# Two k stacks copied from ScalarE's queue, and x's first tile issued ahead of the parameter rows, in a two-layer encoder

## The chip, the cores and the metric

The kernel runs on one core of one Trainium2 chip. The metric is the device time of one execution in microseconds (us). Before the change it is 2428.93 us, the median of three runs (2426.2, 2428.93 and 2428.98).

## The reference, cut to what matters

`h` is 1024 positions by 1024 channels, all float32. Two layers each project `h` to q, k, v (8 heads, two components of 32 channels for q and k, 64 for v) and to u of a Fourier group, attend, mix and normalise, and then run a SwiGLU feed-forward.

```python
h = layer_norm(x, ln_in_g, ln_in_b)
for l in range(DEPTH):                      # DEPTH = 2
    proj = jnp.einsum('bsd,de->bse', h, w_in[l])        # q | k | v | u, 512 columns each
    a = diff_attention(q, k, v, lam, lam_init, subln_g[l])
    f = fourier_mix(u, w_f[l], b_f[l])
    mix = jnp.einsum('bse,ed->bsd', jnp.concatenate([a, f], axis=-1), w_o[l])
    h = layer_norm(ALPHA * h + mix, ln1_g[l], ln1_b[l])
    h = layer_norm(ALPHA * h + swiglu(h, w_gu[l], w_down[l]), ln2_g[l], ln2_b[l])

# diff_attention, for each head: two softmaxes over the same v
s = einsum('bqhcd,bkhcd->bhcqk', q, k) * scale - slope * |qpos - kpos|
p = softmax(s);  a = p[:, :, 0] - lam * p[:, :, 1];  o = a @ v;  o = rms_norm(o) * subln_g * (1 - lam_init)
```

## The kernel before, in words

Every matmul that must keep float32 accuracy is made of three: an operand is split into a high part (`hi`, rounded) and a low part (`lo`, the rest), and `mm3` (L137 to L139) multiplies hi by hi, hi by lo and lo by hi. ScalarE makes `hi`, VectorE or GpSimd makes `lo` by a subtraction (`split`, L127). `hTh` and `hTl` hold the transposed activations.

**The start.** SyncE's queue loads five small parameter rows (`load_rows`, gain and shift of the first norm, b_f, subln_g), then x's first tile in two halves, then four weight tiles of v, then x's other tiles. `spread_ln` (L199) transposes the parameter rows (PE, L201), ScalarE and GpSimd widen two of them (L209, L211), and 16 transposes (L213) spread gain and shift over all partitions in two PSUM tiles. `enter_norm` normalises a tile: statistics on VectorE (L229 to L233), one power on GpSimd (L234), a multiplication by the spread gain out of PSUM on VectorE (L236), a scaling on ScalarE (L238), and the addition of the shift (L240 for tile 0). Each normalised tile is stored to `h_dram` and transposed.

**The first pair of heads in a layer.** `proj_qk` (L293) projects q and k of two heads: PE makes a 128x512 half in a bank `mm`, ScalarE evicts `hi` (tile `st`) and VectorE `lo` (tile `su`). Then it builds stacks: for each of four components `c`, a tile `stk` (q: hi, hi, lo, lo of 32 channels, on 4 x 32 partitions) and a tile `stq` (k: hi, lo, hi, lo), so that one 128-row matmul gives all product terms of a score. (The pool names are crossed: `stk` holds q, `stq` holds k.) Each stack takes four copies of 32 x 1024 float32 (128 KB) from SBUF to SBUF, all issued through `load` (L101, L102), that is by SyncE's queue. In the first pair of layer 0 the stacks of c = 0 and 1 are `stk_708`/`stq_713` and `stk_718`/`stq_723`; in layer 1 they are `stk_11741`/`stq_11746` and `stk_11751`/`stq_11756`.

After k's last half, `proj_v` (L266) makes the last three tiles of v in layer 0 and in layer 1 (24 matmuls of 256 columns each, into a bank `mm`; tiles `mm_748`, `mm_776`, `mm_804` in layer 0, the last one is `mm_11837` in layer 1). There are two `mm` banks, so `mm_804` can begin when `mm_748` has been evicted: ScalarE's cast (L129) and then VectorE's subtraction (L132) for `v_773`.

**Attention.** For each block of 128 queries and each component, `scores` (L387, matmul L392) makes a 128x1024 tile `S` with two 512-column matmuls, `bias_min` adds the ALiBi distance and takes the row's minimum on VectorE (L400), and `expo` takes the exponential on ScalarE (L410). PE fills the time between scores with projections of later pairs (`mm_852` is the first), each step held behind the scores by `tc.issue_after`. Two `S` tiles exist.

**What sets the order.** Each engine runs its instructions in a fixed order, which the build works out from a simulated timeline of all the engines; a queue's DMAs are issued in that order too. The build also hands eight completion counters round to all DMAs of all queues in the scheduled order (`DMAHW0` to `DMAHW7` in the rows of the order below), and a DMA waits until the last one on its counter has landed.

Of the kernel before, what the change touches and what calls it, by code (L numbers as in the profile page):

```python
# [27 lines left out]
HD = 32  # L28
# [31 lines left out]
def f32(t):  # L60
    return t.bitcast(F32)
# [3 lines left out]
def encoder(ctx: ExitStack, tc: tile.TileContext, x, ln_in_g, ln_in_b, w_in, lam_params, subln_g,  # L65
            w_f, b_f, w_o, ln1_g, ln1_b, w_gu, w_down, ln2_g, ln2_b, dist_c, dft_c, grp_c, qsc_c, out):
    nc = tc.nc
# [7 lines left out]
    def nm(s):  # L75
        cnt[0] += 1
        return f"{s}_{cnt[0]}"
# [3 lines left out]
    def blk(tag, shape=(P, 1024), dt=F32):  # L81
        if tag == "s":
            swap[0] ^= 1
            tag = ("su", "st")[swap[0]]
        return sb.tile(list(shape), dt, tag=tag, name=nm(tag), bufs=BUFS[tag])
# [6 lines left out]
    def bank(tag=None):  # L92
        if tag is None:
            alt[0] ^= 1
            tag = ("mm", "tr")[alt[0]]
        return ps.tile([P, 512], F32, tag=tag, name=nm(tag), bufs=2)

    def dbank():
        return ps.tile([P, 1024], F32, tag="S", name=nm("S"), bufs=2)

    def load(o, i):  # L101
        nc.sync.dma_start(out=o, in_=i)  # L102
# [24 lines left out]
    def split(hi, lo, src, hi_eng, lo_eng, note=None):  # L127
        if hi_eng is nc.scalar:
            a = nc.scalar.copy(hi, src)  # L129
        else:  # L130
            a = hi_eng.tensor_copy(out=hi, in_=src)
        b = lo_eng.tensor_tensor(out=lo, in0=src, in1=f32(hi), op=ALU.subtract)  # L132
        if note is not None:
            note[1:] = a, b
# [55 lines left out]
    def load_rows():  # L190
        t = blk("on", (P, P))
        for j, v in enumerate((ln_in_g, ln_in_b)):
            load(t[j * ND:j * ND + ND, :], v.rearrange("(j p) -> j p", p=P))
        load(t[2 * ND:3 * ND, :], b_f.rearrange("l (g p) -> (l g) p", p=P))
        for half in range(2):
            load(t[3 * ND:NR, half * VD:(half + 1) * VD], subln_g)
        return t

    def spread_ln(t):  # L199
        pt = bank("tr")  # L200
        nc.tensor.transpose(pt[:, 0:NR], t[0:NR, :], ident[0:NR, 0:NR])  # L201
        cols = blk("on", (P, NR))
        nc.scalar.copy(cols, pt[:, 0:NR])
        ob, og = dbank(), dbank()
        for k, o in ((0, og), (1, ob)):
            w = blk("stq", (P, ND, P))
            col = cols[:, k * ND:k * ND + ND].unsqueeze(2).broadcast_to([P, ND, P])
            if k:
                nc.gpsimd.tensor_copy(out=w, in_=col)  # L209
            else:  # L210
                nc.scalar.copy(w, col)  # L211
            for j in range(ND):
                nc.tensor.transpose(o[:, j * P:(j + 1) * P], w[:, j, :], ident)  # L213
        b = blk("E")
        nc.scalar.copy(b, ob)
        nc.gpsimd.tensor_copy(out=bfT.rearrange("p l g -> p (l g)"), in_=cols[:, 2 * ND:3 * ND])
        for l in range(DEPTH):
            nc.gpsimd.tensor_scalar(out=subg[:, l:l + 1], in0=cols[:, 3 * ND + l:3 * ND + l + 1],
                                    scalar1=math.sqrt(VD) * (1.0 - LAM_INIT[l]), scalar2=1.0, op0=ALU.mult,
                                    op1=ALU.mult)  # L220
        return og, b, ob
# [34 lines left out]
    def load_v(l):  # L256
        ts = []
        for k in range(4):
            t = blk("E", (P, 2, 2, VH), F32R)
            raw = blk("raw", (P, 2, VH))  # L260
            load(raw, w_in[l, k * 256:(k + 1) * 256, 2 * ATT:2 * ATT + VH].rearrange("(a p) c -> p a c", p=P))
            split(t[:, 0], t[:, 1], raw, nc.scalar, nc.vector if k % 2 and l == 0 else nc.gpsimd)
            ts.append(t)
        return ts
# [12 lines left out]
    def load_w128(l, c0, tag="w"):  # L277
        wh = blk(tag, (P, ND, P), F32R)
        wl = blk(tag, (P, ND, P), F32R)
        for part in range(2):  # L280
            raw = blk("raw", (P, 4, P))
            load(raw, w_in[l, part * 512:part * 512 + 512, c0:c0 + P].rearrange("(a p) c -> p a c", p=P))
            split(wh[:, part * 4:part * 4 + 4, :], wl[:, part * 4:part * 4 + 4, :], raw, nc.scalar, nc.gpsimd)
        return wh, wl

    def proj_t(wh, wl, half, o):
        sl = slice(half * 512, half * 512 + 512)
        for dt in range(ND):
            anchor[1] = mm3(o, wh[:, dt, :], wl[:, dt, :], hTh[:, dt, sl], hTl[:, dt, sl], dt == 0, dt == ND - 1)
            if dt < ND - 1:  # L290
                yield

    def proj_qk(l, pair, stacks):  # L293
        srcs = []
        parts = [(qk, half) for qk in range(2) for half in range(2)]
        if pair == 0:
            parts = [(qk, half) for half in ((1, 0) if l else (0, 1)) for qk in range(2)]
        ready = {}
        for n, (qk, half) in enumerate(parts):
            if qk not in ready:  # L300
                wh, wl = load_w128(l, qk * ATT + pair * P, "aT" if pair == 0 and qk else "w")
                ready[qk] = wh, wl, blk("s", (P, S), F32R), blk("s", (P, S), F32R)
            wh, wl, hi, lo = ready[qk]
            o = bank("mm")
            sl = slice(half * 512, half * 512 + 512)
            yield from proj_t(wh, wl, half, o)
            if qk == 0:
                sc = qsc[:, pair:pair + 1]
                nc.scalar.activation(hi[:, sl], o, AF.Copy, scale=sc)
                nc.vector.scalar_tensor_tensor(out=lo[:, sl], in0=o, scalar=sc, in1=f32(hi[:, sl]),  # L310
                                               op0=ALU.mult, op1=ALU.subtract)
            else:
                split(hi[:, sl], lo[:, sl], o, nc.scalar, nc.vector)
            if n < 3:
                yield "part"
        for qk in range(2):
            wh, wl, hi, lo = ready[qk]
            srcs.append((hi, hi, lo, lo) if qk == 0 else (hi, lo, hi, lo))
        for c in range(4):
            for qk in range(2):  # L320
                t = blk(("stk", "stq")[qk], (P, S), F32R)
                for j in range(4):
                    load(f32(t[j * HD:(j + 1) * HD, :]), f32(srcs[qk][j][c * HD:(c + 1) * HD, :]))
                stacks[qk].append(t)
        yield

# [193 lines left out]
    def attention(l, vs, dist, first):  # L520
# [6 lines left out]
        for h in range(NH):  # L527
            for qt in range(NT):
                if qt % QW == 0:
# [3 lines left out]
                               "z": []})  # L533
                n += 1
        plan = [[proj_qk(l, 1, stacks[1]), proj_vt(l, 2, vs), proj_u(l, 0)],
                [proj_qk(l, 2, stacks[2]), proj_vt(l, 3, vs), proj_u(l, 1)],
                [proj_qk(l, 3, stacks[3]), proj_u(l, 2)],
                [fourier(l)]]
        hs = []
# [556 lines left out]
    rs = [blk("v") for _ in range(NT)]  # L1096
    for i in range(NT):
        if i == 0:
            rows_ = load_rows()
            for c in (slice(0, D // 2), slice(D // 2, D)):  # L1100
                load(rs[i][:, c], x[i * P:(i + 1) * P, c])
            gb = spread_ln(rows_)
            wv = load_v(0)
        else:
            load(rs[i], x[i * P:(i + 1) * P, :])
# [94 lines left out]
```

## Time and profile before

| | |
|---|---|
| median of three runs | 2428.93 us (2426.2 to 2428.98) |
| the profiled execution | 2429.76 us |
| its span, first to last instruction | 2427.5 us |
| mean granted TensorE clock | 0.988 |
| PE busy | 2339.9 us, 96% of the span |
| VectorE, GpSimd, ScalarE busy | 1850.9, 1809.8, 1212.5 us |
| DMA moved | 187.60 MB, mean 77 GB/s |

PE, PEld, DVE, ACT, POOL and SP are TensorE's matmuls, its weight loads, VectorE, ScalarE, GpSimd and SyncE. A time in a row is counted from the first instruction of the span. An L and a number is the line of the kernel. In a timeline, the bracket at the end is the idle time of that engine ahead of the instruction, and what ended it. The granted clock is 1.00 at 2.4 GHz and 0.50 at 1.2 GHz.

### The profile page before, as it was taken

How to read it: one execution, taken by the hardware profiler on the slowest of the kernel's cores; microseconds unless marked ns; L12 is line 12 of the kernel's file. 1: busy time of each engine (PE TensorE's matmuls, PEld its weight loads, DVE VectorE, ACT ScalarE, POOL GpSimd, SP SyncE). 2: the span in 40 equal slices, each digit the busy share in tenths (PEclk: the TensorE clock that was granted, in tenths of full speed). 3: DMA queues.
4: the chain of work that ended last, by engine and by line, in shares of the span. 5: the costliest groups of instructions: out<-in, count | busy, mean ns of one | idle time of the engine just before them, and what ended most of it. 6: DMA issues, size and time to landing. Idle time of an engine off the chain costs nothing.

```text
span 2427.5 us, 33266 instructions
## 1 busy us (share of the span) xinstructions
PE 2339.9 (96%) x11649; PEld 1947.2 (80%) x11649; DVE 1850.9 (76%) x2930; ACT 1212.5 (50%) x2203; POOL 1809.8 (75%) x1378
## 2 busy tenths in 40 slices
PE   7999998999999999999999999989999999999997
PEld 6888876777888888888788888777878888888886
DVE  6587888556688888888768788884566888888878
ACT  4577777524343343434437777774243343434442
POOL 4476778656798888888535777784678888888873
PEclk9999999999999999999999999999999999999999
DMA  6542242421121111121324233325011211111112
GB/s 236 144 102 65 75 105 101 115 81 48 44 61 53 57 53 57 53 61 53 102 87 102 74 77 94 113 66 174 14 53 47 62 58 57 53 57 53 53 35 100
DMA packets 187919, 187.60 MB, mean 77 GB/s; under 512 B 24912, under 2 KB 148200, under 8 KB 187752
## 3 DMA queue, kind: packets, MB, share of 16 engines
q1 hardware_dynamic: 187752, 185.47, 26.2%
q8 instruction: 93, 1.52, 0.3%
q14 instruction: 74, 0.61, 0.1%
HBM read 128.01 MB, written 23.86 MB: 63 GB/s over the span
## 4 chain that ended last, share of the span: by engine, by line
PE 81%; DVE 8%; issue 3%; POOL 3%; ACT 2%; DMA 2%; SPq 1%; DVEq 0%; POOLq 0%; ACTq 0%
PE mm L137 10%; PE mm L139 10%; PE mm L138 10%; PE S L137 7%; PE S L138 7%; PE S L139 7%; PE tr L137 6%; PE tr L139 6%; PE tr L138 6%; PE mm L450 4%; PE S L392 4%; PE tr L428 3%; DVE E L400 2%; DVE v L183 1%; DVE aT L440 1%
## 5 line engine op out<-in xcount | busy, mean ns | idle before, releaser
L1012 DVE TENSOR_TENSOR v<-S,v 128x512 f32<-128x512 f32 x504 | 333.5, 684 | 42.9 <-PE S L139 42.9
L400 DVE CUSTOM_DVE_ANT_0 E<-S,dist 128x1024 f32<-128x1024 f32 x256 | 309.4, 1217 | 48.0 <-PE S L392 28.1
L410 ACT ACTIVATE E<-E,mn 128x1024 f32<-128x1024 f32 x256 | 296.0, 1157 | 85.3 <-DVE mn L400 84.1
L420 POOL TENSOR_TENSOR E<-E,E 128x1024 f32<-128x1024 f32 x110 | 263.9, 2401 | 4.2
L419 POOL TENSOR_SCALAR E<-E,rho 128x1024 f32<-128x1024 f32 x110 | 123.9, 1127 | 156.8 <-DVE rho L416 122.4
L137 PE MATMUL S<-w,st 128*128 128x512 f32 x544 | 212.1, 390 | 0.7 <-ACT w L129 0.7
L138 PE MATMUL S<-w,st 128*128 128x512 f32 x544 | 211.6, 389 | 0.0
L139 PE MATMUL S<-w,st 128*128 128x512 f32 x544 | 211.3, 389 | 0.0
L132 POOL TENSOR_TENSOR stk<-raw,stk 128x512 fp32r<-128x512 f32 x138 | 196.0, 1421 | 19.8 <-ACT stk L129 17.1
L132 POOL TENSOR_TENSOR st<-stq,st 128x512 fp32r<-128x512 f32 x126 | 194.8, 1547 | 13.4 <-ACT st L129 10.9
L899 DVE TENSOR_TENSOR su<-su,tr 128x512 f32<-128x512 f32 x176 | 116.4, 681 | 114.5 <-PE tr L139 111.0
L440 DVE TENSOR_TENSOR aT<-tr,aT 128x512 fp32r<-128x512 f32 x256 | 172.5, 683 | 37.8 <-ACT aT L435 37.3
L137 PE MATMUL mm<-hTh,w 128*128 128x512 f32 (+1 forms) x448 | 183.5, 409 | 5.7 <-ACT w L129 2.3
L435 ACT CAST aT<-tr 128x512 fp32r<-128x512 f32 x256 | 148.8, 586 | 66.5 <-PE tr L428 50.9
L392 PE MATMUL S<-stq,stk 128*128 128x512 f32 x512 | 165.1, 413 | 17.3 <-DVE mn L400 12.8
L129 ACT CAST stk<-raw 128x512 fp32r<-128x512 f32 x138 | 85.4, 619 | 177.5 <-PE tr L139 113.8
L139 PE MATMUL mm<-hTh,w 128*128 128x512 f32 (+1 forms) x448 | 173.7, 388 | 0.0
L132 POOL TENSOR_TENSOR stk<-dist,stk 128x512 fp32r<-128x512 f32 x88 | 115.7, 1315 | 76.9 <-ACT stk L129 76.8
L138 PE MATMUL mm<-hTl,w 128*128 128x512 f32 (+1 forms) x448 | 172.7, 385 | 0.0
L428 PE MATMUL tr<-ident,E 128*128 128x128 f32 x1024 | 153.8, 275 | 6.7 <-DVE aT L440 6.4
L129 ACT CAST stk<-dist 128x512 fp32r<-128x512 f32 x90 | 56.1, 623 | 207.5 <-PE tr L139 123.2
L132 POOL TENSOR_TENSOR stk<-on,stk 128x512 fp32r<-128x512 f32 x88 | 123.3, 1401 | 44.2 <-ACT stk L129 44.2
(354 smaller groups left out, 6985.9 us busy)
## 6 DMA issues: line engine op xcount, KB each, us to landing
on<-in_w_gu SPq DMA_DIRECT2D x88, 256.0 KB, 2.9
raw<-in_w_gu SPq DMA_DIRECT2D x88, 256.0 KB, 2.9
raw<-in_w_in SPq DMA_DIRECT2D x64, 256.0 KB, 3.1
stq<-in_w_down SPq DMA_DIRECT2D x36, 256.0 KB, 2.9
stk<-st SPq DMA_DIRECT2D x64, 128.0 KB, 2.4
stk<-su SPq DMA_DIRECT2D x64, 128.0 KB, 2.5
stq<-st SPq DMA_DIRECT2D x64, 128.0 KB, 2.4
stq<-su SPq DMA_DIRECT2D x64, 128.0 KB, 2.5
```

Of the source, the lines that this page charges most:

```text
L132: b = lo_eng.tensor_tensor(out=lo, in0=src, in1=f32(hi), op=ALU.subtract)
L137: nc.tensor.matmul(o, ah, bh, start=start, stop=False, skip_group_check=more)
L138: nc.tensor.matmul(o, ah, bl, start=False, stop=False, skip_group_check=more)
L139: return nc.tensor.matmul(o, al, bh, start=False, stop=stop, skip_group_check=more)
L392: anchor[0] = nc.tensor.matmul(s[:, half * 512:half * 512 + 512], qs[:, qt * P:qt * P + P], ks[:, half * 512:half * 512 + 512], start=True ...
L400: nc.vector.tensor_tensor_reduce(out=e, in0=s, in1=blk_["dist"][:, 896 - P * qt:896 - P * qt + S], op0=ALU.add, op1=ALU.min, scale=2.0 ** ...
L410: nc.scalar.activation(e, e, AF.Exp, bias=blk_["mn"][c], scale=-1.0, accum_out=blk_["z"][c])
L420: nc.gpsimd.tensor_tensor(out=es[0], in0=es[0], in1=es[1], op=ALU.add)
L428: anchor[0] = nc.tensor.transpose(pt[:, j, :], blk_["e"][0][:, c0:c0 + P], ident)
L435: nc.scalar.copy(grp["aT"][kh][0][:, :, qq * P:qq * P + P], blk_["pt"][kh])
L440: nc.vector.tensor_tensor(out=lo[:, :, qs], in0=blk_["pt"][kh], in1=f32(hi[:, :, qs]), op=ALU.subtract)
L1012: nc.vector.tensor_tensor(out=dst, in0=o, in1=dst, op=ALU.add)
```

## The change

The eight copies of the stacks `stq` of c = 0 and c = 1 in each layer's first pair (k's first two stacks) are issued by ScalarE's queue in place of SyncE's. The two half loads of x's first tile are issued in front of the five parameter rows. Below the first piece of the diff all lines are one further down in the kernel after.

```diff
--- before.py
+++ after.py
@@ -319,8 +319,9 @@
         for c in range(4):
             for qk in range(2):
                 t = blk(("stk", "stq")[qk], (P, S), F32R)
+                queue = nc.scalar if pair == 0 and qk and c < 2 else nc.sync
                 for j in range(4):
-                    load(f32(t[j * HD:(j + 1) * HD, :]), f32(srcs[qk][j][c * HD:(c + 1) * HD, :]))
+                    queue.dma_start(out=f32(t[j * HD:(j + 1) * HD, :]), in_=f32(srcs[qk][j][c * HD:(c + 1) * HD, :]))
                 stacks[qk].append(t)
         yield
 
@@ -1096,9 +1097,9 @@
     rs = [blk("v") for _ in range(NT)]
     for i in range(NT):
         if i == 0:
-            rows_ = load_rows()
             for c in (slice(0, D // 2), slice(D // 2, D)):
                 load(rs[i][:, c], x[i * P:(i + 1) * P, c])
+            rows_ = load_rows()
             gb = spread_ln(rows_)
             wv = load_v(0)
         else:
```

The build's order of the instructions moves with it. On ScalarE, in layer 0, between k's last eviction (`st_542`) and the evictions of v, the order before (in brackets the counters and engines that an instruction waits for) is:

```order
L129 CAST st_542<-mm_681 128x512 [waits PE_49]
L129 CAST v_773<-mm_748 128x2x2x64 [waits DMAHW2_49,PE_49]
L129 CAST v_801<-mm_776 128x2x2x64 [waits DMAHW3_49,PE_49]
L129 CAST v_829<-mm_804 128x2x2x64 [waits DMAHW4_49,PE_49,Pool_49]
```

And the order now, in the same place:

```order
L129 CAST st_542<-mm_681 128x512 [waits PE_49]
L324 DMA stq_713<-st_542 32x1024 [waits DMAHW0_49,DMAHW5_49,DVE_49,Activation_49]
L324 DMA stq_713<-su_543 32x1024 [waits DMAHW7_49,DVE_49]
L324 DMA stq_713<-st_542 32x1024 [waits DMAHW1_49]
L324 DMA stq_713<-su_543 32x1024 [waits DMAHW3_49]
L324 DMA stq_723<-st_542 32x1024 [waits DMAHW5_49,DMAHW2_49]
L324 DMA stq_723<-su_543 32x1024 [waits DMAHW7_49]
L324 DMA stq_723<-st_542 32x1024 [waits DMAHW1_49]
L324 DMA stq_723<-su_543 32x1024 [waits DMAHW3_49]
L129 CAST v_773<-mm_748 128x2x2x64 [waits PE_49]
L129 CAST v_801<-mm_776 128x2x2x64 [waits PE_49]
L411 ACTIVATE E_838,z_122_833<-E_838,mn_837 128x1024 [waits DVE_49]
```

Eight copies stand ahead of the casts of `v_773` and `v_801`, each with a wait for a counter, and the exponential of the first block stands ahead of the cast of `v_829` (one row further). Layer 1 has the same eight copies ahead of the cast of `v_11806`.

On PE, where v's last tile `mm_804` stood ahead of the first pair of score matmuls `S_834` (a piece of the difference, layer 0):

```order
 L138 MATMUL mm_776<-E_150,hTh 128x256
 L139 MATMUL mm_776<-E_150,hTl 128x256
+L393 MATMUL S_834<-stq_713,stk_708 128x512 x2
 L137 MATMUL mm_804<-E_135,hTh 128x256
 L138 MATMUL mm_804<-E_135,hTh 128x256
@@ -309,9 +310,8 @@
 L138 MATMUL mm_804<-E_150,hTh 128x256
 L139 MATMUL mm_804<-E_150,hTl 128x256
-L392 MATMUL S_834<-stq_713,stk_708 128x512 x2
 L137 MATMUL mm_852<-hTh,w_840 128x512
 L138 MATMUL mm_852<-hTl,w_840 128x512
 L139 MATMUL mm_852<-hTh,w_841 128x512
```

The first score pair moved in front of the 24 matmuls of `mm_804`. In layer 1 `S_11867` moved in front of `mm_11837` in the same way.

On VectorE, the reduction of the first scores (a piece of the difference, layer 0):

```order
 L310 SCALAR_TENSOR_TENSOR su_504<-mm_654,qsc,st_503 128x512
 L132 TENSOR_TENSOR su_543<-mm_681,st_542 128x512
+L401 ISA E_838,mn_837<-S_834,dist_613 128x1024
+L401 ISA mn_837 128x1
 L132 TENSOR_TENSOR v_773<-mm_748,v_773 128x2x128
 L132 TENSOR_TENSOR v_801<-mm_776,v_801 128x2x128
 L132 TENSOR_TENSOR v_829<-mm_804,v_829 128x2x128
-L400 ISA E_838,mn_837<-S_834,dist_613 128x1024
-L400 ISA mn_837 128x1
```

The reduction of `S_834` moved in front of the subtractions for `v_773`, `v_801` and `v_829`. In layer 1 the reduction of `S_11867` moved in front of the subtraction for `v_11806` likewise. What else differs on these engines is swaps of near neighbours, almost all of them in the first 70 us of the program. SyncE's order has the transfer `t_dram<-stq_649` (384 KB) one place earlier, ahead of the copies to `stk_708`.

## Rows read from the trace of the kernel before

**Rows 1.** The page: busy us of each engine (share of the span).
```profile
PE 2339.9 (96%) x11649; PEld 1947.2 (80%) x11649; DVE 1850.9 (76%) x2930; ACT 1212.5 (50%) x2203; POOL 1809.8 (75%) x1378
```

**Rows 2.** Windows: us, busy us of PE, PEld, DVE, ACT, POOL; clock, DMA share, GB/s.
```profile
88.00:150.00 62.00, 61.93 (x331) 52.45 (x332) 51.35 (x104) 45.38 (x86) 40.40 (x25) 0.97 0.36 83
1262.00:1300.00 38.00, 38.00 (x211) 33.02 (x210) 18.77 (x38) 19.72 (x35) 14.93 (x10) 1.00 0.56 126
```

**Rows 3.** Waits of PE: total us, times, longest us.
```profile
PE S L392 <- DMA stq<-su: 3.5, 2, 2.7
```

**Rows 4.** Timeline of SP (start us, us), layer 0, 70:88.
```profile
74.21 0.54 SPq L102 DMA_DIRECT2D t_dram<-stq  x1
...
76.79 2.74 SPq L102 DMA_DIRECT2D stk<-st  x2
79.62 0.55 SPq L102 DMA_DIRECT2D stq<-st  x1
```

**Rows 5.** Chain that ended last, 66:100.
```profile
77.38 2.15 SPq L102
...
85.29 2.64 DMA stq<-su
```

**Rows 6.** DMA issues of 70:90: KB each, median us to landing.
```profile
stq<-su SPq DMA_DIRECT2D x5, 128.0 KB, 2.4
...
t_dram<-stq SPq DMA_DIRECT2D x1, 384.0 KB, 4.3
```

**Rows 7.** Timeline of PE, layer 0, 78:93 [idle before <-releaser].
```profile
80.16 0.28 PE L137 MATMUL mm<-E,hTh 128*128 128x256 f32 x1
...
84.01 0.70 PE L392 MATMUL S<-stq,stk 128*128 128x512 f32 x2 [0.80 <-DMA stq<-su]
...
88.07 1.15 PE L392 MATMUL S<-stq,stk 128*128 128x512 f32 x2 [2.67 <-DMA stq<-su]
...
91.56 0.39 PE L137 MATMUL mm<-hTh,w 128*128 128x512 f32 x1
```

**Rows 8.** Timeline of DVE, layer 0, 74:90.
```profile
83.69 0.42 DVE L132 TENSOR_TENSOR v<-mm,v 128x256 fp32r<-128x256 f32 x1 [2.44 <-ACT v L129]
84.87 1.23 DVE L400 CUSTOM_DVE_ANT_0 E<-S,dist 128x1024 f32<-128x1024 f32 x1 [0.75 <-PE S L392]
```

**Rows 9.** Windows of 2 us around the wait, layer 0.
```profile
86.00:88.00 2.00, 0.00 (x0) 0.00 (x0) 0.10 (x2) 1.24 (x2) 0.00 (x0) 1.00 0.98 223
88.00:90.00 2.00, 1.93 (x5) 1.57 (x6) 0.65 (x1) 0.00 (x0) 0.00 (x0) 0.53 0.93 203
90.00:92.00 2.00, 2.00 (x7) 1.57 (x6) 0.59 (x2) 1.24 (x2) 0.00 (x0) 0.62 0.93 201
```

**Rows 10.** Timeline of PE, layer 1, 1273:1284.
```profile
1276.76 0.28 PE L137 MATMUL mm<-E,hTh 128*128 128x256 f32 x1
...
1279.63 0.63 PE L392 MATMUL S<-stq,stk 128*128 128x512 f32 x2
1280.10 0.39 PE L137 MATMUL mm<-hTh,w 128*128 128x512 f32 x1
```

**Rows 11.** Timeline of SP, layer 1, 1266:1280.
```profile
1271.81 0.51 SPq L102 DMA_DIRECT2D stq<-st  x1
```

**Rows 12.** Windows of 2 us, DMA share and GB/s in layer 1, then layer 0.
```profile
1272.00:1274.00 2.00, 2.00 (x19) 2.00 (x19) 0.51 (x1) 0.00 (x0) 0.00 (x0) 1.00 0.90 195
...
72.00:74.00 2.00, 2.00 (x11) 1.65 (x10) 0.00 (x0) 0.00 (x0) 1.98 (x2) 1.00 1.02 399
```

**Rows 13.** Timelines of SP, PE and DVE at the program's start.
```profile
0.72 0.40 SPq L102 DMA_DIRECT2D on<-in_ln_in_g  x1
...
2.43 0.83 SPq L102 DMA_DIRECT2D v<-in_x  x2
...
5.09 3.68 PE L213 MATMUL S<-ident,stq 128*128 128x128 f32 x16 [1.35 <-ACT stq L211]
...
7.32 1.39 DVE L236 SCALAR_TENSOR_TENSOR v<-v,bmv,S 128x512 f32<-128x512 f32 x2
```

## The prediction

> **What bounds the kernel now.** I read the page first: PE is busy 2339.9 us of the span, 96% [rows 1], so a change pays only where PE stands idle or runs at the lower clock, and costs where it makes PE wait. I then took the two places that the stacks touch, as windows. After them, in 88 to 150 us and 1262 to 1300 us, PE is busy 61.93 of 62 us and 38.00 of 38 us [rows 2]: it has no slack, so what is lost or won at either place stays until the end. The table of PE's waits gives what the copies cost now: scores waiting for a copy to `stq`, 3.5 us in two waits, the longer 2.7 us [rows 3].
>
> The timelines say where. In layer 0 `mm_804` starts at 80.16; the first score pair runs at 84.01 after 0.80 us of waiting, the second at 88.07 after 2.67 us [rows 7]. SyncE issues ten copies from 79.62 to 85.29 [rows 4, 5], one every 0.63 us, and the last one needs 2.64 us to land [rows 5]. The waits cost clock as well: PE did nothing in 86 to 88 us and was granted 0.53 and 0.62 in the next two windows [rows 9], between the two levels 1.2 and 2.4 GHz. PE's 3.93 busy us there at a mean of 0.575 lost some 1.7 us. In layer 1 there is no such wait: `mm_11837` starts at 1276.76 and the scores follow at 1279.63 without a gap [rows 10].
>
> **The change, part by part.**
>
> *SyncE loses 16 issues.* At 0.63 us each that is 5 us for each layer, and it is what the first layer could win. But the order moves the first score pair ahead of the last tile of v, to where PE is at 80.16 in layer 0 and at 1276.76 in layer 1. And VectorE has the reduction of those scores ahead of the subtraction that frees the bank of `mm_804` (`mm_11837`). So where 24 matmuls covered the copies there is now a wait, and behind the scores a second one. The second is sized by rows: scores to reduction 84.01 to 84.87, 0.86 us, the reduction 1.23 us and the subtraction 0.42 us [rows 7, 8]: 2.5 us from the start of the score pair to the start of the 24 matmuls, of which the pair itself is 0.47 at full clock (1279.63 to 1280.10 [rows 10]). The subtraction's own cast has long been possible on ScalarE, but stands behind all eight copies; the last copy waits for the fourth's landing and then takes about 0.6 us, so the cast, 0.4 us like the subtraction that follows it, is done about 1 us after the scores start and hides behind the reduction.
>
> *Layer 0.* ScalarE's first copy waits on the counter of `t_dram<-stq_649`. That transfer was issued at 74.21 and took 4.3 us to land [rows 4, 6]; it now goes some 2 us earlier and lands at about 76.4. The fourth waits on the counter of the second copy to `stk_718`, now issued at 77.38, with SyncE held 2.15 us by it [rows 5], up to 79.53. So the fourth copy leaves at 79.6 to 81.3. Landing takes 2.4 us [rows 6], or up to 4 if both queues share the engines: 82.0 to 85.3, middle 83.6; 80.6 is the best conceivable (the issue's 2.15 us being no delay of the data). With scores at 83.6, `mm_804` starts at 86.1, ends 2.9 us later (24 matmuls, 1276.76 to 1279.63 [rows 10]) at 89.0, and three matmuls, the second score pair and six more (0.7 + 0.47 + 1.4, at half the pair's time for each) reach 91.5. Idle for 3.4 and 2 us in a row, PE falls to the lower clock as before: 1.6 us more, 93.1. The same point was reached at 91.56 [rows 7]. **Layer 0: +1.5 us**, bounds -3.0 (scores at 80.6, no clock lost: 88.5) and +3.4 (85.3).
>
> *Layer 1.* The first copy can leave at 1271.8, as now [rows 11]; the fourth waits for the landing of the second copy to `stk_11751` and leaves at about 1273.8 (three issues later). SyncE goes on at the same time with the later stacks. The DMA engines are 0.90 busy at 195 GB/s with one queue's copies [rows 12]. If that share is their limit, two queues with four copies each in flight need 8 x 0.6 = 4.8 us (0.6 being the pace of one queue at that share) for a landing in place of 2.4, and the fourth lands at about 1278.4. If it is not (the same engines moved 399 GB/s with wider transfers at share 1.02 [rows 12]), it lands at 1276.2, before PE wants it. I take 1278.4, since the row of this very kind of copy is the nearest. Scores at 1278.4 put `mm_11837` at 1280.9; without any wait it would be at 1276.76 + 0.47 = 1277.2. That is 3.7 us, and two idle stretches of 1.6 and 2 us bring the lower clock, 1.6 us by the loss in layer 0. **Layer 1: +5.3 us**, bounds +2.0 (only the wait behind the reduction, 2.5 - 0.47, which nothing hides) and +7.
>
> The Trainium skill (DMA: Bandwidth & Descriptors, section "Issuing engines are not separate DMA queues") says that DMAs of all issuing engines run on the same 16 DMA engines and interleave, so that a second issuer saves only issue time. By that rule layer 1 is the +5.3 us; without it, it would be +2.0. The share of 0.90 agrees; no run yet has two issuers.
>
> *The start.* SyncE's first issue, now a parameter row, leaves at 0.72; x's halves take 0.83 us [rows 13] and go first. The rows then leave 0.88 us later, and their chain (transposes L213 from 5.09 for 3.68 us) must give the gain before VectorE's L236, now at 7.32 [rows 13]; L213's first eight, half of its 3.68 us, are through at about 6.9. So L236 moves to about 7.8: **+0.5 us**. Below: x's data come up to 1.7 us earlier (-1.7 if the rows never matter); above: small rows queue behind 512 KB of x, +1.5.
>
> *The rest* of the order is swaps of neighbours; I cost them at nothing, as PE's stretches around them stay full. Other copies on SyncE come earlier, and nothing waits for them [rows 2].
>
> The sum is 0.5 + 1.5 + 5.3 = +7.3 us on the profiled execution's 2429.76, or 2437.1. That execution is 0.83 us over the median of 2428.93, so the forecast for the median is **2436.2 us**.
>
> **The rivals.**
>
> *1. Layer 0's stacks arrive in time (not slower).* The mechanism is SyncE's serial issue, up to 85.29 [rows 5], cut in two queues. It decides at the landing of the fourth copy: at about 80.6 scores follow `mm_776` directly, no lower clock is granted, and layer 0 gains 3.0; layer 1 then also lands in time, at its floor of +2.0. With the start 0.5: -0.5, **2428.4 us**. For it: the engines carried twice the bytes. Against it: the wait for the second copy to `stk_718` [rows 5].
>
> *2. The engines carry both queues, but layer 0's waits remain.* 0.5 + 1.5 + 2.0 = +4.0: **2432.9 us**. It decides in layer 1, at a landing before 1276.76 and a clock that holds.
>
> *3. The issues of the two queues take turns.* One issue of 2.15 us [rows 5] shows that an issue can be held up. If each of ScalarE's copies waits out one of SyncE's, they leave every 1.25 us: in layer 0 the fourth leaves at about 81.5 and the scores come at 85, +2.9; in layer 1 it leaves at 1276.8, lands at 1279.3, and `mm_11837` starts at 1281.8: 4.6 + 1.6 = +6.2. With 0.5 that is +9.6: **2438.5 us**. The Trainium skill (Perfetto Trace Analysis, section "DMA Instruction — HWDGE (DVE, Sync)") describes a descriptor generator locked for one sequencer's use, which would do this; no row here shows two sequencers at it.
>
> *4. Changes of order elsewhere gain more than any row prices:* a gain over 5 us, say **2423 us**. No stretch of PE's row promises it.
>
> That the change does not do what it says is out: sixteen copies stand on ScalarE in the order.
>
> **How the numbers follow.** A measurement of this kernel tells some 0.2%, 4.9 us, from no change. The forecast has 0.39 and rival 3 0.18, both slower by more than that: 0.57. Rival 2 has 0.18 and rival 1 0.16, both within it: 0.34. Rival 4 has 0.09. Rival 1 with the start's best (-1.7) gives 2426.2, and the upper bounds (1.5 + 3.4 + 7) give 2440.8. The range 2427.2 to 2441 takes in the forecast, rivals 1 to 3 and leaves out rival 4 and the ends.
>
> **What would show it.** Right: PE waiting ahead of the first score pair in both layers, for a copy issued by ScalarE, some 3.4 and 1.6 us; then some 2 us ahead of `mm_804` and `mm_11837`, released by VectorE; a granted clock below 1 after both; landings near 5 us in layer 1; L236 near 7.8. Wrong: landings of 2.4 us with two queues busy (rival 2), issues of over 1 us on both queues (rival 3), a first score pair directly behind `mm_776` (rival 1), or `mm_11837` starting right after the scores, which would break the largest term.

## The result, and the profile after

The changed kernel takes 2439.29 us, the median of four runs (2436.49 to 2443.16), beside 2428.7 us before in the same comparison (2426.2 to 2428.98). The ratio is 1.0052, with a 95% interval of 1.0041 to 1.0064: slower by 12.6 us of 2428.7 (10.0 to 15.5). Slower was forecast, but at +7.3 us; 2428.93 us times the ratio is 2441.6 us, just over the upper end of the range, 2441.0.

The profiled execution took 2443.16 us, the longest of the four. Its span, and the line of its page that answers to [rows 1]:

```profile
span 2441.2 us, 33275 instructions
...
PE 2343.1 (96%) x11649; PEld 1949.7 (80%) x11649; DVE 1849.4 (76%) x2930; ACT 1213.3 (50%) x2203; POOL 1809.5 (74%) x1378
```

PE did the same work in 3.2 us more of busy time, and the span grew by 13.7 us, so the rest is idle time. In layer 0, PE's timeline, which answers to [rows 7]:

```profile
85.17 1.19 PE L393 MATMUL S<-stq,stk 128*128 128x512 f32 x2 [2.65 <-DMA stk<-st]
88.23 0.55 PE L137 MATMUL mm<-E,hTh 128*128 128x256 f32 x1 [1.87 <-DVE v L132]
...
93.22 0.63 PE L393 MATMUL S<-stq,stk 128*128 128x512 f32 x2
...
95.72 0.62 PE L393 MATMUL S<-stq,stk 128*128 128x512 f32 x2
```

PE waits 2.65 us ahead of the first score pair, and again 1.87 us, behind VectorE's subtraction for v, ahead of `mm_804`. The second pair needs no wait any more. ScalarE's timeline at the same place, first before the change, then now (ACTq rows are DMA issues):

```profile
74.61 0.59 ACT L129 CAST st<-mm 128x512 fp32r<-128x512 f32 x1 [3.88 <-PE mm L139]
77.48 0.37 ACT L129 CAST v<-mm 128x256 fp32r<-128x256 f32 x1 [2.29 <-PE mm L139]
```

```profile
76.80 0.59 ACT L129 CAST st<-mm 128x512 fp32r<-128x512 f32 x1 [3.90 <-PE mm L139]
77.48 0.59 ACTq L324 DMA_DIRECT2D stq<-st  x1
...
79.20 0.73 ACTq L324 DMA_DIRECT2D stq<-st  x1
81.68 0.51 ACTq L324 DMA_DIRECT2D stq<-su  x1
...
84.99 0.59 ACTq L324 DMA_DIRECT2D stq<-su  x1
85.62 0.65 ACT L129 CAST v<-mm 128x256 fp32r<-128x256 f32 x2 [8.23 <-DMA stq<-st]
```

The cast of `v_773`, which before ran 2.9 us after k's last eviction had started (77.48 after 74.61), stands behind eight copies, from 77.48 to 85.58, and runs at 85.62, 8.8 us after it. (The bracket names a landing of a copy; by the order above, the cast itself waits for PE alone, which was long done.) VectorE's reduction of the first scores ended later than that cast:

```profile
86.51 1.22 DVE L401 CUSTOM_DVE_ANT_0 E<-S,dist 128x1024 f32<-128x1024 f32 x1 [8.40 <-PE S L393]
```

The clock, two of the windows that answer to [rows 9], and one in layer 1:

```profile
86.00:88.00 2.00, 0.36 (x1) 0.00 (x0) 1.49 (x3) 0.48 (x2) 0.00 (x0) 0.50 1.05 234
88.00:90.00 2.00, 1.77 (x8) 1.80 (x9) 0.41 (x2) 1.02 (x2) 0.00 (x0) 0.50 0.97 213
```

```profile
1288.00:1290.00 2.00, 1.65 (x8) 1.68 (x9) 0.53 (x2) 1.41 (x3) 0.00 (x0) 0.50 1.05 211
```

Layer 1, which had no wait at all [rows 10], on PE:

```profile
1285.63 0.96 PE L393 MATMUL S<-stq,stk 128*128 128x512 f32 x2 [2.49 <-DMA stk<-su]
1288.35 0.55 PE L137 MATMUL mm<-E,hTh 128*128 128x256 f32 x1 [1.75 <-DVE v L132]
...
1296.45 0.62 PE L393 MATMUL S<-stq,stk 128*128 128x512 f32 x2
```

and the landings there (KB each, median us), first of ScalarE's four copies from `su`, then of the one issued at 1280.13, the fourth that ScalarE issues, beside the DMA share and GB/s of one window:

```profile
stq<-su ACTq DMA_DIRECT2D x4, 128.0 KB, 5.0
```

```profile
stq<-su ACTq DMA_DIRECT2D x1, 128.0 KB, 5.5
```

```profile
1278.00:1280.00 2.00, 2.00 (x19) 2.00 (x19) 0.69 (x1) 0.01 (x1) 0.00 (x0) 1.00 1.03 217
```

A copy from ScalarE's queue takes 5.0 us to land (the profile has two of the four landings, 4.6 and 5.5) where 2.4 us was usual [rows 6], at 217 GB/s and a share of 1.03, against 195 GB/s and 0.90 with one queue [rows 12]: these two queues move hardly more than one. The brackets of the two first score pairs name copies to `stk`, which SyncE issues. The landing shows that PE waited for ScalarE's copy all the same: in layer 1 the fourth was down 5.5 us after 1280.13, at 1285.6, where the pair starts. In layer 0 the counter of the fourth, issued at 81.68, reached its last step at 84.97, and the pair starts at 85.17.

The start, PE before and now, and VectorE now, which answer to [rows 13]:

```profile
3.47 0.27 PE L201 MATMUL tr<-ident,on 26*128 26x26 f32 x1 [3.47 <-DMA on<-in_subln_g]
```

```profile
5.14 0.27 PE L201 MATMUL tr<-ident,on 26*128 26x26 f32 x1 [5.14 <-DMA on<-in_subln_g]
6.76 3.67 PE L213 MATMUL S<-ident,stq 128*128 128x128 f32 x16 [1.35 <-ACT stq L211]
```

```profile
3.41 1.40 DVE L229 BATCH_NORM_STATS2 bst<-v 128x6 f32<-128x512 f32 x2 [3.41 <-DMA v<-in_x]
...
8.77 1.41 DVE L236 SCALAR_TENSOR_TENSOR v<-v,bmv,S 128x512 f32<-128x512 f32 x2 [3.53 <-PE S L213]
```

x's statistics begin at 3.41 us, but the parameter rows are transposed at 5.14 in place of 3.47, and L236 comes at 8.77 in place of 7.32.

To see where the time went, I take three marks in each trace: the multiplication L236, k's last eviction in a layer (ScalarE's cast to `st`), and the third score pair, which stands behind all the disputed waits. They divide the program into a start, a stretch for each layer, and the rest. All in us:

| kernel | L236 | k's last eviction, layer 0 | from there to the third pair, layer 0 | the same, layer 1 | ratio to before, interval |
|---|---|---|---|---|---|
| before | 7.32 | 74.61 | 17.65 | 12.09 | 1 |
| after | 8.77 | 76.80 | 18.92 | 19.02 | 1.0052 (1.0041 to 1.0064) |
| e1, x first alone | 8.91 | 76.71 | 12.96 | 12.08 | 0.9984 (0.9972 to 0.9995) |
| e2, copies alone | 7.45 | 75.80 | 21.44 | 17.96 | 1.0050 (1.0037 to 1.0063) |
| e3, copies of layer 0 alone | 7.30 | 74.76 | 21.15 | 12.09 | 1.0015 (1.0006 to 1.0024) |
| e4, copies of layer 1 alone | 7.11 | 74.49 | 16.99 | 18.68 | 1.0022 (1.0013 to 1.0031) |
| e5, after with the order of before | 8.82 | 75.47 | 17.68 | 18.48 | 1.0042 (1.0030 to 1.0055) |
| e6, before, tables first | 7.12 | 75.54 | 15.15 | 12.09 | 1.0002 (0.9993 to 1.0011) |
| e7, before, tables last | 7.15 | 75.75 | 12.52 | 12.08 | 0.9998 (0.9990 to 1.0007) |
| e8, after with one stack | 8.88 | 76.71 | 13.30 | 12.18 | 0.9997 (0.9988 to 1.0006) |
| e9, e5 on GpSimd's queue | 9.14 | 76.36 | 13.97 | 12.86 | 1.0002 (0.9993 to 1.0010) |

After against before: start +2.2 us, layer 0 +1.3, layer 1 +6.9, together 10.4, near the 10.6 between the medians. The other 3.3 us of this execution's span lie outside the three stretches. Most of it falls between the layers; one part can be seen in a window near 360 us, where the granted clock fell in this execution

```profile
358.00:360.00 2.00, 2.00 (x10) 1.90 (x10) 2.00 (x5) 0.82 (x3) 2.00 (x3) 0.50 0.92 201
```

and did not in the execution before at the same place in time:

```profile
358.00:360.00 2.00, 2.00 (x14) 1.78 (x14) 2.00 (x5) 1.42 (x3) 1.34 (x3) 1.00 0.87 261
```

The runs of one kernel lie up to 13 us apart (e1, 2420.4 to 2433.3). How much of that such falls make is not shown; single traces are compared by stretches here.

### The profile page after: what moved, and what is told of

The parts are those of the page before. It is cut to its first block, busy times and chain, and to the rows that moved or that the text cites. A ratio compares the mean times of both kernels' runs of the same rounds, so it can differ in the third digit from the quotient of the medians.

```text
span 2441.2 us, 33275 instructions
## 1 busy us (share of the span) xinstructions
PE 2343.1 (96%) x11649; PEld 1949.7 (80%) x11649; DVE 1849.4 (76%) x2930; ACT 1213.3 (50%) x2203; POOL 1809.5 (74%) x1378
## 4 chain that ended last, share of the span: by engine, by line
PE 80%; DVE 8%; ACT 3%; DMA 3%; POOL 2%; issue 2%; SPq 1%; DVEq 0%; POOLq 0%; ACTq 0%
PE mm L137 10%; PE mm L138 10%; PE mm L139 10%; PE S L137 7%; PE S L138 7%; PE S L139 7%; PE tr L137 6%; PE tr L138 6%; PE tr L139 6%; PE mm L451 4%; PE S L393 3%; PE tr L429 3%; DVE E L401 2%; ACT E L411 1%; DVE aT L441 1%
```

## The experiments

**e1 and e2: each half of the change alone.** e1 keeps x's tile ahead and puts the copies back; e2 does the opposite.

```diff
--- after.py
+++ e1_x_first.py
-                queue = nc.scalar if pair == 0 and qk and c < 2 else nc.sync
+                queue = nc.sync
```

> The change with the sixteen copies back on SyncE: only x's first tile goes ahead of the parameter rows. The theory (each part has its own cost, and they add up) expects +2.2 us against the kernel before: L236 of the first tile near 8.8 us in place of 7.3, k's last eviction of layer 0 (the cast of st) near 76.8 in place of 74.6, and layer 1 without a wait for a copy. Rival: layer 0's wait for the copies hides the late start, since the copies do not depend on it; then the time is within 0.5 us of before.

> The change with the parameter rows back in front of x: only the sixteen copies on ScalarE's queue. The theory expects +1.3 us in layer 0 and +6.9 us in layer 1, +8.2 us in all, and a start as before (L236 at 7.3). Rival (the whole loss comes from the late start, which shifts the order of everything behind it): below +3 us.

e1 took 2423.95 us, ratio 0.9984: faster than both kernels, by 3.9 us than before. Its start is as late as that of the whole change (k's last eviction +2.1), and layer 0 more than gives it back. PE's timeline of e1:

```profile
85.14 0.63 PE L393 MATMUL S<-stq,stk 128*128 128x512 f32 x2
...
87.08 0.69 PE L393 MATMUL S<-stq,stk 128*128 128x512 f32 x2 [0.61 <-DMA stq<-su]
```

The first pair waits for nothing and the second 0.61 us, where before they waited 0.80 and 2.67 [rows 7], and no lower clock follows. So the theory had the start right and the sum wrong, and the rival fell short too: layer 0's wait hid the late start, and there was more to win. Of the 4.7 us that its stretch of layer 0 is shorter, 2.1 are the late start, which the copies did not share; 1.0 is the second pair, which comes that much earlier (87.08 for 88.07); and 1.6 are the clock, which did not fall behind it (2.59 us from the second pair to the third, for 4.19). The stretches together win 2.6 us, and the interval of the time allows 1.2 to 6.8. e2 took 2440.82 us, 1.0050 or +12.1 us (9.0 to 15.3): the copies carry the whole loss, against +8.2 expected. Its layer 0 lost 3.8 us and its layer 1 5.9 by the table, and its start 1.2, in which the order of the first 70 us differs; that cause was not tested.

**e3 and e4: the copies in one layer alone** (rows ahead of x, as before).

```diff
--- e2_copies.py
+++ e3_layer0.py
-                queue = nc.scalar if pair == 0 and qk and c < 2 else nc.sync
+                queue = nc.scalar if l == 0 and pair == 0 and qk and c < 2 else nc.sync
```

e4 has `l == 1` in the same place.

> Rows in front of x, and only layer 0's eight copies on ScalarE's queue. The theory expects +1.3 us: a wait ahead of the first score pair and one ahead of mm_804, in place of the two waits of before; layer 1 as before. Rival (layer 0 gains by the second queue, and the loss is all in layer 1): -3 to 0 us.

> Rows in front of x, and only layer 1's eight copies on ScalarE's queue. The theory expects +6.9 us: PE waits some 2.5 us ahead of the first score pair and 1.8 us ahead of the last tile of v, and runs at the lower clock behind it; copies take some 5 us to land with both queues busy. Rival (only the wait behind the reduction, the engines carry both queues): +2 us, landings of 2.4 us.

e3: 1.0015, +3.6 us (1.5 to 5.8), of which layer 0's stretch shows 3.5; the theory had 1.3. e4: 1.0022, +5.3 us (3.2 to 7.5), with 6.6 in layer 1's stretch. Both layers lose, and neither rival holds. Layer 0's own loss is larger than in the whole change, since there the late start hides part of it: copies cost 18.92 - 12.96 = 6.0 us against e1, and the other half of the change had won 4.7.

**e5: is it the order?** The scores are held behind the last tile of v, on PE and so on VectorE, as before the change.

```diff
--- after.py
+++ e5_order.py
+    last_v = [None]
...
-            mm3(o, hTh[:, dt, sl], hTl[:, dt, sl], w[:, 0, dt % 2, :], w[:, 1, dt % 2, :], dt == 0, dt == ND - 1)
+            last_v[0] = mm3(o, hTh[:, dt, sl], hTl[:, dt, sl], w[:, 0, dt % 2, :], w[:, 1, dt % 2, :], dt == 0, dt == ND - 1)
...
-            anchor[0] = nc.tensor.matmul(s[:, half * 512:half * 512 + 512], qs[:, qt * P:qt * P + P],
-                                         ks[:, half * 512:half * 512 + 512], start=True, stop=True)
+            with tc.issue_after(last_v[0].ins) if last_v[0] else nullcontext():
+                anchor[0] = nc.tensor.matmul(s[:, half * 512:half * 512 + 512], qs[:, qt * P:qt * P + P],
+                                             ks[:, half * 512:half * 512 + 512], start=True, stop=True)
+            last_v[0] = None
```

> The changed kernel with one rule added: the first score pair of each layer is issued behind the last tile of v, as before the change (and with it VectorE's reduction behind the subtractions for v). Theory A (the loss is the order: scores put ahead of 24 matmuls that had covered the copies): both layers lose their waits, and the time falls to that of the first tile's move alone, about 2424 to 2427 us. Theory B (the queue itself costs: ScalarE's casts of v are held behind eight copies whose landings take 5 us with both queues busy, so the bank of the last tile of v comes free late in any order): PE waits some 4 us ahead of the last tile of v in layer 1 in place of 2.5 and 1.8, the time stays within 3 us of the changed kernel's.

2438.39 us, 1.0042: theory B. PE, and ScalarE's queue, in layer 1:

```profile
1284.04 0.58 PE L137 MATMUL mm<-E,hTh 128*128 128x256 f32 x1 [3.61 <-DVE v L132]
```

```profile
1274.72 0.59 ACT L129 CAST st<-mm 128x512 fp32r<-128x512 f32 x1 [3.90 <-PE mm L139]
...
1277.46 0.63 ACTq L326 DMA_DIRECT2D stq<-su  x1
1278.60 0.51 ACTq L326 DMA_DIRECT2D stq<-st  x1
...
1282.55 0.51 ACTq L326 DMA_DIRECT2D stq<-su  x1
1283.16 0.65 ACT L129 CAST v<-mm 128x256 fp32r<-128x256 f32 x2 [7.86 <-DMA stq<-st]
```

and the landing of the fourth copy there, the one issued at 1277.46:

```profile
stq<-su ACTq DMA_DIRECT2D x1, 128.0 KB, 5.1
```

The two waits of the changed kernel have become one, of 3.61 us, ahead of the last tile of v. The cast of v runs at 1283.16, 7.9 us after k's last eviction ended, because the fifth to eighth copy wait for the landing of the first four: the fourth landed 5.1 us after 1277.46, and the eighth was issued at 1282.55. The last tile of v reads no copy, so this wait is the cast's alone. The order takes only 0.5 us of layer 1's 6.9 (19.02 against 18.48) and 1.2 of layer 0's.

**e6 and e7: layer 0's tables.** e1's gain had an order in it: with x ahead, the last transfer of the tables that are kept in `t_dram` (`t_dram<-stq_649`) is issued ahead of all stack copies. e6 makes that order alone, from the kernel before; e7 puts all four transfers behind the first two stacks.

```diff
--- before.py
+++ e6_tfirst.py
-                    load(f32(t[j * HD:(j + 1) * HD, :]), f32(srcs[qk][j][c * HD:(c + 1) * HD, :]))
+                    with tc.issue_after(kept[0].ins) if l == 0 and pair == 0 else nullcontext():
+                        load(f32(t[j * HD:(j + 1) * HD, :]), f32(srcs[qk][j][c * HD:(c + 1) * HD, :]))
...
-                load(t_dram[part][:, c0:c1], f32(t))
+                kept[0] = load(t_dram[part][:, c0:c1], f32(t))
```

```diff
--- before.py
+++ e7_tlast.py
+                if l == 0 and pair == 0 and qk and c == 1:
+                    with tc.issue_after(copy.ins):
+                        for args in later:
+                            load(*args)
...
-                load(t_dram[part][:, c0:c1], f32(t))
+                later.append((t_dram[part][:, c0:c1], f32(t)))
```

> The kernel before (rows first, all copies on SyncE) with one rule added: layer 0's stack copies are issued behind the last transfer of the tables to t_dram (384 KB), the order that the build chose by itself when x's first tile went ahead. Theory (in the run with x's tile alone, layer 0 gained 4.7 us by this order alone and lost 2.1 us at the start): -4.7 us, PE's wait for a copy 0.6 us or less in place of 3.5, no lower clock behind it, L236 at 7.3. Rival (the gain there came from the late start, which gave the copies' backlog 2 us to drain, not from the order): 0 to -2.5 us.

> The kernel before with layer 0's four transfers to t_dram (1.8 MB) issued behind the copies of the first two stacks, in place of in front and between. If the backlog of these transfers is what delays the copies, PE's waits for a copy go to zero in layer 0: -5.2 us (3.5 us of waits and 1.7 us of clock), as far as or a little beyond the run with the tables first. If the pace of SyncE's issues (0.63 us each) is what counts, the second score pair still waits over 1.5 us.

e6: 1.0002. Its layer 0 is 2.5 us shorter, but its k comes 0.9 us later, and its second pair comes when it came before and still waits:

```profile
88.07 0.69 PE L395 MATMUL S<-stq,stk 128*128 128x512 f32 x2 [2.78 <-DMA stq<-su]
```

```profile
88.00:90.00 2.00, 1.93 (x9) 1.61 (x10) 1.10 (x1) 0.00 (x0) 0.00 (x0) 1.00 0.92 199
```

So the order by itself brought the second pair's copies no earlier, and the theory fell. Of the 2.5 us, 0.9 are PE's late arrival, as e6's rival has it, and 1.6 the clock: behind 2.78 us of waiting, with none ahead of the first pair, it stayed at 1.00 in this execution, where it was 0.53 before, behind 0.80 and 2.67 us [rows 9]. e7 does what was expected in its place, no wait ahead of either pair:

```profile
84.18 0.63 PE L398 MATMUL S<-stq,stk 128*128 128x512 f32 x2
...
85.66 0.69 PE L398 MATMUL S<-stq,stk 128*128 128x512 f32 x2
```

5.1 us won in layer 0's stretch, of which 1.1 are lost at k's eviction; yet the time is that of before, 0.9998. The traces show where the other 4 us go. Waits of PE for VectorE in 100 to 345 us (total us, times, longest), before and in e7:

```profile
PE S L392 <- DVE mn L400: 0.8, 2, 0.5
```

```profile
PE S L398 <- DVE mn L406: 3.4, 7, 1.3
PE tr L434 <- DVE aT L446: 2.6, 4, 1.1
```

The row's minimum holds the scores 2.6 us longer than before, and the transposes to `aT` 1.3 us longer (1.3 before): in layer 0's attention PE waits for VectorE for what it had won. e6 has 3.1 us of the first kind, and e1 has 0.8, as before, and keeps its gain. Why the build's order of VectorE's work came out worse in e6 and e7 stays open.

**e8: half the copies; e9: another queue.** These take apart what e5 left together: casts held on ScalarE, and the rate of the DMA engines with two queues.

```diff
--- after.py
+++ e8_one_stack.py
-                queue = nc.scalar if pair == 0 and qk and c < 2 else nc.sync
+                queue = nc.scalar if pair == 0 and qk and c < 1 else nc.sync
```

```diff
--- e5_order.py
+++ e9_gpsimd.py
-                queue = nc.scalar if pair == 0 and qk and c < 2 else nc.sync
+                queue = nc.gpsimd if pair == 0 and qk and c < 2 else nc.sync
```

> The changed kernel with half the copies: only the first k stack (c = 0, four copies for each layer) goes to ScalarE's queue, and the build's order then leaves the first scores behind the last tile of v. If ScalarE's queue is held mainly by the second four copies, each of which waits for one of the first four to land, the casts of v come in time (just behind the fourth copy's issue): layer 1 loses nothing (in place of 6.9 us), layer 0 no more than 1 us against the run with x's tile alone, and the time is 2422 to 2427 us. If any copy on ScalarE's queue costs its share, half of the loss stays: 2429 to 2433 us.

> The run with the order of before kept, with the sixteen copies on GpSimd's queue in place of ScalarE's, so that nothing of v is held behind them and no copy waits for another's landing; both queues are busy all the same. If ScalarE's held casts are the cost, PE waits no more ahead of the last tile of v, and the time is within 3 us of the run with x's tile alone (some 2422 to 2427 us). If the rate of the DMA engines is the cost, the second score pair of layer 1 waits some 3 us for its copies and the time stays above 2430 us. GpSimd's own time for issuing them is not known from any row; it has no other work there in layer 0.

e9, layer 1, PE, the landings and a window:

```profile
1278.29 0.70 PE L396 MATMUL S<-stq,stk 128*128 128x512 f32 x2 [0.15 <-DMA stk<-su]
...
1279.80 0.70 PE L396 MATMUL S<-stq,stk 128*128 128x512 f32 x2
```

```profile
stq<-su POOLq DMA_DIRECT2D x4, 128.0 KB, 5.3
```

```profile
1274.00:1276.00 2.00, 2.00 (x19) 2.00 (x18) 0.29 (x1) 0.37 (x1) 0.43 (x1) 1.00 0.97 287
```

The copies land as slowly as from ScalarE's queue, 5.3 us (4.0 those from `st`), and PE waits 0.15 us all the same: layer 1's loss falls from 6.4 us (e5) to 0.8. Slow landings alone cost little, since all the copies were issued within some 4 us of k's eviction and held nothing else. The cost in e5 was ScalarE's queue standing still behind its copies' counters, and PE waited there for the cast. But e9 frees more than the casts: its engines moved 287 GB/s, more than the 217 of ScalarE's and SyncE's queues together, and no copy of the second stack waits for a landing. In e5 the last of those was issued at 1282.55 and took 4.9 us, while the second pair, by its distance of before, could have run at some 1284.3 (an estimate: 1280.80 - 1271.20 us behind k's eviction at 1274.72); without the held cast PE would have waited some 3 us there. No run frees the casts and nothing else. e8 shows the queue from the other side. ScalarE in layer 1:

```profile
1267.49 0.59 ACT L129 CAST st<-mm 128x512 fp32r<-128x512 f32 x1 [3.89 <-PE mm L139]
...
1270.61 1.32 ACTq L324 DMA_DIRECT2D stq<-su  x1
1272.03 0.37 ACT L129 CAST v<-mm 128x256 fp32r<-128x256 f32 x1 [3.95 <-DMA stq<-st]
```

The fourth copy is issued at 1270.61 and the cast follows at 1272.03, before PE needs its bank: layer 1 is back at 12.18. Its scores stand behind the last tile of v too, as in e5 and e9, so no run has the new order with a free cast. Both kernels are level with before (0.9997 and 1.0002) and some 12 us faster than the changed one. By its stretches e8 wins 2.2 us, like e1; its interval, -2.9 to +1.5 us, allows that and does not show it. Their times, 2427.23 and 2428.22 us, are at the upper end of what was expected or a little over it.

**e10 and e11: the parameter rows on ScalarE's queue,** from e8 and from e7, to have x and the rows both early.

```diff
--- e8_one_stack.py
+++ e10_rows_act.py
-            load(t[j * ND:j * ND + ND, :], v.rearrange("(j p) -> j p", p=P))
+            nc.scalar.dma_start(out=t[j * ND:j * ND + ND, :], in_=v.rearrange("(j p) -> j p", p=P))
```

The other three rows are changed alike, and e11 makes the same edit in e7, with x ahead.

> The run with one stack on ScalarE's queue, and the five parameter rows issued by ScalarE's queue too, beside x's halves on SyncE's. If the 2.1 us lost at the start come from the rows standing behind x on one queue, L236 comes at 7.3 or earlier (8.8 before), and k's last eviction of layer 0 at 74.6 or earlier. If layer 0's scores are then bound by the copies (the second pair has come at 87 to 88 us in nearly every order), PE waits there instead and the total stays within 2 us of the run with one stack: 2423 to 2427 us. If not, 2421 to 2423 us. Rival: rows and x share the DMA engines, so two queues bring the rows no earlier: L236 at 8 or later.

> All copies on SyncE, layer 0's transfers to t_dram behind the first two stacks, and the five parameter rows on ScalarE's queue beside x's halves. This takes away the late start and the copies' backlog together: L236 at 7.3 or earlier, no wait for a copy ahead of the first two score pairs of layer 0 (or under 1 us), the first of them near 83 us. Against before, -5 us at 100 us if both add. In the run with the tables last the gain of layer 0 was gone by 450 us; if that repeats, the total is within 3 us of before.

1.0019 (1.0011 to 1.0028) and 1.0027 (1.0016 to 1.0039): both slower, and further off than e10's rival had it. The start of e10 on PE, and two pieces of the chain that ended last there (start us, us, what):

```profile
7.05 0.27 PE L201 MATMUL tr<-ident,on 26*128 26x26 f32 x1 [7.05 <-DMA on<-in_subln_g]
```

```profile
0.72 2.99 DMA v<-in_x
...
3.73 3.13 DMA on<-in_subln_g
```

Four rows are issued from 0.73 to 2.31 us. The fifth leaves only at 3.73: its counter is that of x's first half, which had to land first. It then took 3.1 us to land beside x and w_in, for 2.0 in the changed kernel, and PE could transpose only at 7.05. L236 came at 10.7 us, and in e11 its like at 10.5. e11's second score pair waits 2.46 us, where under 1 us was expected.

## Why the prediction was wrong in size

The three terms were to add up to 7.3 us and measured 10.4 in the traces: the start was 1.7 us short, layer 1 1.6 us, and layer 0 came out right by luck. The ratio's 12.6 us are some 2 more, from outside the three stretches, where the forecast had nothing and the traced execution 3.3; why is not shown.

- **Places.** Right: waits ahead of the first score pair in both layers, for ScalarE's fourth copy (2.65 and 2.49 us, for 3.4 and 1.6 forecast), then ahead of `mm_804` and `mm_11837` behind VectorE (1.87 and 1.75 us, for some 2), a lower clock after both, no gap in PE's work behind them.
- **The start, +0.5 us,** was mis-sized. L236 moved by 1.5 us, which I had as the upper bound (small rows behind 512 KB of x), and k's last eviction by 2.2. I had moved the rows by the 0.88 us of x's issues alone. In the chain of waits, the last row took 2.0 us to land behind x, and the wait ahead of L201 grew from 3.5 to 5.1 us, by 1.7. The other 0.7 us up to k's eviction belong to what I called the rest and put at nothing.
- **Layer 0, +1.5 us,** measured +1.3, but as the difference of two terms that I did not have: 6.0 lost by the copies, 4.7 won by x's move (e1). I had seen that `t_dram<-stq_649` goes earlier, and used it only to date ScalarE's first copy. That a late start is hidden where PE waits for copies anyway was not in my sum: e1 shows it. So the agreement of 1.3 with 1.5 is luck.
- **Layer 1, +5.3 us,** measured +6.9. Of the 1.6 us more, 1.0 is the first pair, which came later mainly because the fourth copy took 5.5 us to land where the sum had some 4.6 (its 1273.8 and 4.8 make 1278.6 besides, not 1278.4); the rest is 0.2 behind the reduction and 0.4 of clock. The step that failed is the one that named the cause: the order of scores and matmuls, with the cast of v hidden "behind the reduction". e5 takes the order back and gains 0.5 us of the 6.9; e8 and e9, with the order of before as well, free ScalarE's queue and gain nearly all of it. In the changed kernel the casts were indeed done at 86.27 us (85.62 and 0.65), before the reduction ended at 87.7, so the wait ahead of `mm_804` ended as I said; but without the order the cast itself would have held PE nearly as long. Two causes stood in parallel, and I priced one. What the order costs with a free cast was not run.
- **Landings.** 5.0 us with two queues, as taken (4.8). With the order of before and nothing held behind the copies, landings as slow cost layer 1 only 0.8 us (e9). The Trainium skill (DMA: Bandwidth & Descriptors, "Issuing engines are not separate DMA queues") has DMAs of all issuers interleave on the same engines; the trace agrees, 217 GB/s at share 1.03 against 195 at 0.90.
- **Rivals.** 1 and 2 fell with the landings. 3 fell too: issues on ScalarE's queue took 0.51 to 0.73 us, so they took no turns with SyncE's; what spaced them was waiting for counters. Its mechanism is not ruled out: in e8, issues that overlap in layer 1 took 1.04 and 1.32 us on ScalarE's queue and 1.34 and 1.28 on SyncE's. Its price for layer 1 counted four spacings of 1.25 us where three lie between the first copy and the fourth, which makes it 1.3 us too dear. Rival 4 found its gain in e1, not in the change.
- **The range** holds the median of the four runs, 2439.29 us, but not 2441.6, the ratio's. Its upper end was the sum of upper bounds, and the start had been bounded at L236 only.

## What to carry to other kernels

A DMA moved to another engine's queue brings its waits along: read what compute stands behind it on that engine, and how many of its transfers must land before the last one can be issued. Moving half as many copies, or using a queue with nothing behind it, cost nothing here (with the order of before), where the full move cost 0.5%. Ahead of a stage that waits for DMA anyway, a late start can be free: the part of the change that looked worst at the start was the one that made the kernel faster (e1, 0.9984, at most 0.9995). And a gain in one stage counts only if the next stage keeps it: e7 won 4 us and gave them back in waits for VectorE.

## What had not been expected

- x's tile ahead of the parameter rows delays the first norm by 1.6 us (8.91 against 7.32) and yet wins 3.9 us (1.2 to 6.8) in all: layer 0's stretch is 4.7 us shorter.
- Five rows of a few KB on ScalarE's queue, beside x and w_in on SyncE's, were usable at 7.05 us, against 3.47 us on one queue ahead of x and 5.14 us behind x. A counter shared with x's first half held the last of them up to 3.73 us.
- The rate of these 32-partition copies stays at 182 to 248 GB/s, in windows of 2 us of layer 1, with SyncE's queue alone or with ScalarE's beside it, where wider transfers had 399 GB/s [rows 12]. With GpSimd's queue beside SyncE's it reached 287 GB/s (e9), with landings just as slow. Why is not shown.
